# Six column groups of the projections put ahead of attention, and the row blocks in another order

## The chip, the core and the metric

The kernel runs on one core of a Trainium2 chip. The metric is the device time of one execution in microseconds, the median of the runs shown. The engines are TensorE (PE in the profile; PEld are its weight loads), VectorE (DVE), ScalarE (ACT), GpSimd (POOL) and SyncE (SP), which here only issues DMAs; 16 DMA engines move data.

## What is computed

One step of a hybrid decoder layer for a prompt of 1024 tokens and eight tokens to decode. The input is normed and projected; the columns of the projection go to three mixers (sparse attention, causal pooling, a chunked gating MLP), each has a SiLU gate, and one output projection follows.

```python
q, kc, ks, kw, gl, za, pin, zb, u, v, zc = project(rms_norm(xp, norm_pre[l]), w_in[l])
ya = nsa_attend(q, gates, kc, ks, kw, ...)          # compressed + selected + window branches, ALiBi
yb = pool_mix(pin, zeros, 0, pool_w[l], pool_scale[l])
yc, vn = gmlp_mix(u, v, gmlp_norm[l], gmlp_ws[l], gmlp_bs[l], CHUNK)
mix = concat([ya * silu(za), yb * silu(zb), yc * silu(zc)])
xp = xp + rms_norm(mix @ w_out[l], norm_post[l])
```

The same is done for the eight decoded tokens against paged caches.

## The kernel before

All arithmetic that needs float32 precision is done in float16 halves: a value is held as a high part and a low part, and each product is three matmuls (high by high, low by high, high by low).

**Column groups.** `tgroup(gi, ...)` (L538) projects 128 columns of w_in for all 1032 tokens: three pieces (344 tokens each) of 24 matmuls. Its `prefetch` makes the halves of the next group's weights (`split_w`, L255 on ScalarE; the low half at L261 on VectorE, or at L258 and L259 on GpSimd once attention has begun) and loads those of the group after (`load_w`, L243, on SyncE; one `raw` buffer). After a group its `post_...` steps run on the other engines: `post_silu` (gates), `post_u` and `gmlp` (the MLP, with matmuls of its own), `post_pin` (pooling, mostly on GpSimd; it loads `dsh` from the pool state at L1126, copies the last eight columns into it on ScalarE at L1162 and stores it by `o_ps` at L1163) and `poolmm`.

**Stages.** The first 250 us hold the projections for attention and the decoding of the eight tokens, in which `weave` alternates chunks of a group with chunks of side work. Then comes attention over the prompt. Six groups are left for it: ZC1, U1, PIN1, ZB1, PIN0 and ZB0.

**Attention.** A row block is 128 queries; block i has 8 heads and needs i + 1 tiles of keys in the selected branch and up to 5 in the window. A unit is one head (of blocks 7 to 3), two (2, 1) or four (0). For each unit: scores on TensorE (tile s), the table and the row maximum on VectorE (L1344, tile P), exp on ScalarE (L1346), the high half H (L1348, ScalarE), the low half L (L1362, VectorE), a transposing DMA for each half on SyncE (L1355 for H, L1363 for L, both into tile T), and three units later the product with the values on TensorE (tile O). There are 2 buffers each of P, H and L, and 3 of T. When a block's eight heads are through, `combine` and `finish` merge the branches, a transposing DMA puts the result into `qa` (L1432), and `outproj` (tiles op) multiplies it by w_out: 48 matmuls of 512 columns for each block.

**What sets the order.** The loop over units asks `take` for fill: chunks of `side` and `fill` on TensorE, as many as a budget from PARAM's s1 and s2 allows. `fill` holds the six groups in turn, then `early_wo` and `open_out`, which free the projections' memory and load and split w_out (`load_wo` L1467 on GpSimd, `split_wo` L1492 and L1493), then the output projections. `side` holds the MLP, the pooling matmuls and `dec_out`, the output projection of the decoded tokens (tiles dops, do, dor). A scheduler orders the instructions of TensorE, VectorE and ScalarE; SyncE and GpSimd issue in the order of the program (`manual_schedule`). Each engine works through its own instructions in order.

Of the kernel before, what the change touches and what calls it, by code (L numbers as in the profile page):

```python
# [42 lines left out]
NCE = _lay(CE, [("ident", 128), ("bones", 128), ("tril", 128), ("oneh", 8), ("td", 520), ("tcd", 64),  # L43
                ("gsel", 24), ("nsl", 1)])
NCD = _lay(CD, [("gpre", 8), ("gpost", 8), ("psc", 2), ("gn", 2), ("ws0", 2), ("bs0", 2)])
PARAM = {"s1": 6.2, "s2": 0.52, "banks": 2, "gp": "-", "p0": 4.0, "p1": 4.0, "p2": 3.0, "p3": 2.5, "lone": 2, "lsp": -1, "tw": 512}
NCX = 128 + 256 + 256


# [1 line left out]
def tile_hymba(ctx: ExitStack, tc: tile.TileContext, A: dict):  # L51
# [54 lines left out]
    now = [0.0]  # L106
# [431 lines left out]
    def tgroup(gi, scale, post, raw=False):  # L538
        while busy(2):
            yield 0, None  # L540
        grab()
        prefetch(gi)
        ws = wsp[gi]
        t = t32(f"t{gi}")
        for c in range(3):
            ps = fp.tile([128, 512], F32, tag="f", name=f"ps{gi}_{c}")[:, :CH]
            for k in range(8):
                t_mms(ps, ws, c, k, k == 0, k == 7)

            def done(c=c, ps=ps):  # L550
                if raw:
                    S.activation(t[:, c * CH:c * CH + CH], ps, AF.Copy, scale=scale)
                else:
                    evac(t, ps, c, scale)
                if c == 2:
                    return fin() if raw else post(t)

            def fin():
                while "R" not in hold:
                    yield  # L560
                V.tensor_tensor(t, t, R, ALU.mult)
                post(t)
            yield 3.5, done
# [27 lines left out]
    def prep(kind, b):  # L591
# [3 lines left out]
        S.activation(hl[:, 0], xf, AF.Copy)  # L595
        (G if kind in PARAM["gp"] else V).tensor_tensor(hl[:, 1], xf, hl[:, 0], ALU.subtract)
        chl[kind, b] = hl
# [440 lines left out]
    def dec_mix():  # L1038
        need("zd0", "zd1", "zd2", "zd3")
        t = yzd  # L1040
        for k in range(2):
            a = k * 64
            V.tensor_tensor(t[a:a + 64], oda[a:a + 64].rearrange("p (b k g) -> p k g b", k=2, g=4)[:, k],
                            yzd[a:a + 64], ALU.mult)
        V.tensor_scalar(t, t, 2.0 ** -11, None, ALU.mult)
        hilo(md[:, 0], md[:, 1], t)
        yield 0, None


    def post_silu(nm):  # L1050
        def f(t):
            while busy():
                yield
            grab()
            y = t32(f"y{nm}")
            S.activation(y, t, AF.Tanh, scale=0.5)
            yield
            if nm[1] == "b":
                V.scalar_tensor_tensor(y, y, 1.0, t, ALU.add, ALU.mult)
            else:  # L1060
                G.tensor_scalar(y, y, 1.0, None, ALU.add)
                G.tensor_tensor(y, y, t, ALU.mult)
                yield from until(later(4.0))
            grab(-1)
            yield
            hold[nm] = y
        return f

    def post_u(f2):
        def f(t):  # L1070
            while f"zc{f2}" not in hold:
                yield
            G.tensor_tensor(t, t, hold.pop(f"zc{f2}"), ALU.mult)  # L1073
            grab(-1)
            yield from until(later(2.3))
            hold[f"w{f2}"] = t
        return f

    def gmlp(f2):
        yield from wait("vn", f"w{f2}")  # L1080
        while busy():
            yield 0, None
        grab()
        yc = t32(f"yc{f2}")
        def fin():
            V.tensor_scalar(yc[:, 1024:NT], vnd[:, f2], ccd("ws0")[:, f2:f2 + 1], ccd("bs0")[:, f2:f2 + 1],
                            ALU.mult, ALU.add)
            G.tensor_tensor(yc, yc, hold.pop(f"w{f2}"), ALU.mult)
            grab(-1)
            yield from until(later(2.3))  # L1090
            yield
            m = mxg[f2] = C.tile([128, 2, NT], F16, tag=f"mxg{f2}", name=f"mxg{f2}")
            S.activation(m[:, 0], yc, AF.Copy)
            G.tensor_tensor(m[:, 1], yc, m[:, 0], ALU.subtract)
            grab(-1)
            yield from until(later(3.3))
            hold[f"mxg{f2}"] = 1

        for h in range(2):
            ps = fp.tile([128, 4, 128], F32, tag="f", name=f"gp{f2}{h}")  # L1100
            for n4 in range(4):
                n = h * 4 + n4
                for a, b in ((0, 0), (1, 0), (0, 1)):
                    for g2 in range(2):
                        g = f2 * 2 + g2
                        mm(ps[g2 * 64:g2 * 64 + 64, n4], vnh[:, a, n, g * 64:g * 64 + 64],
                           wst[:, b, g * 128:g * 128 + 128], a + b == 0, b == 1)

            def done(h=h, ps=ps):
                y4 = yc[:, h * 512:h * 512 + 512].rearrange("p (n i) -> p n i", i=128)  # L1110
                V.scalar_tensor_tensor(y4, ps, 1.0 / 64, bst[:, f2].unsqueeze(1).to_broadcast([128, 4, 128]),
                                       ALU.mult, ALU.add)
                if h == 1:
                    return fin()
            yield 1.4, done
# [65 lines left out]
    def poolmm(f2):  # L1181
        yield from wait(f"dh{f2}", f"zb{f2}")
        mxp = hold["mx"]
        hl = mxp[:, f2]
        y = hold.pop(f"zb{f2}")
        w = wpl[:, :, f2 * 128:f2 * 128 + 128]
        def fin():
            S.activation(mxp[:, f2, 0], y, AF.Copy)
            G.tensor_tensor(mxp[:, f2, 1], y, mxp[:, f2, 0], ALU.subtract)
            grab(-1)  # L1190
            yield from until(later(3.3))
            hold[f"mxp{f2}"] = 1

        for c in range(3):
            ps = fp.tile([128, 512], F32, tag="f", name=f"pp{f2}{c}")[:, :CH]
            c0 = c * CH
            mm(ps, w[:, 0], hl[:, 0, c0:c0 + CH], True, False)
            mm(ps, w[:, 0], hl[:, 1, c0:c0 + CH], False, False)
            mm(ps, w[:, 1], hl[:, 0, c0:c0 + CH], False, True)

            def done(c=c, c0=c0, ps=ps):
                V.scalar_tensor_tensor(y[:, c0:c0 + CH], ps, psc2[:, f2:f2 + 1], y[:, c0:c0 + CH],
                                       ALU.mult, ALU.mult)
                if c == 2:
                    return fin()
            yield 0.45, done
# [10 lines left out]
    def weave(main, side, per):  # L1217
        owed = 0.0
        while True:
            c = chunk(main)  # L1220
            if c is None:
                return
            bg_step()
            if copies and now[0] > 75:
                cwin_copy(*copies.pop(0))
            owed += c
            while side and owed >= per:
                owed -= per
                if chunk(side[0]) is None:
                    side.pop(0)  # L1230
                    continue
                bg_step()
# [11 lines left out]
    for n in range(32):  # L1244
        page(n // 4, n % 4)
    side = [small(), dec_cmp()]
    weave(tgroup(G_KWV, 1.0 / 64, lambda t: post_v(1, t), raw=True), side, PARAM["p0"])
    for g in range(4):
        weave(group_q(g), side, PARAM["p1"])
    flush()  # L1250
# [30 lines left out]
    def load_qx(i, hf):  # L1281
        t = qx[i, hf] = AT.tile([128, 2, 128], F16, tag="qx", name=f"qx{i}{hf}", bufs=2)
        for k in range(2):
            Y.dma_start(t[64 - k * 64:128 - k * 64], qa[k * 64:k * 64 + 64, i, hf * 4 + k:hf * 4 + 4:2])

    ROWS = (7, 6, 2, 1, 0, 5, 4, 3)
    load_qx(ROWS[0], 0)

    def spans(i):
        n = min(i + 1, 5)  # L1290
# [148 lines left out]
    def open_out():  # L1439
        X.release()  # L1440
        outp["O"] = tc.alloc_tile_pool(name="O", bufs=1, side="left", reuse_waits="tile")
        outp["one"] = outp["O"].tile([128, 128], F32, name="one2")
        G.memset(outp["one"], 1.0)
        bg.append(split_wo())
        yield 0.1, None

    def early_wo():
        load_wo(0)
        yield 0.1, None
# [173 lines left out]
        units += [(i, s, nh) for s in range(0, 8, nh)]  # L1623
    fill = []

    side = []

    def take(budget):
        banks = 0
        c = 0  # L1630
# [10 lines left out]
        while budget > 0 and fill and banks < PARAM["banks"]:  # L1641
# [4 lines left out]
            if c == 0:  # L1646
# [2 lines left out]
            budget -= c  # L1649
        return min(budget, 0.0)  # L1650

    fill += [tgroup(G_ZC1, 1.0 / 64, post_silu("zc1")), tgroup(G_U1, 1.0 / 128, post_u(1)),
             tgroup(G_PIN1, 1.0 / 64, post_pin(1)), tgroup(G_ZB1, 1.0 / 64, post_silu("zb1")),
             tgroup(G_PIN0, 1.0 / 64, post_pin(0)), early_wo(), tgroup(G_ZB0, 1.0 / 64, post_silu("zb0")),
             open_out()]
    side += [dec_mix(), gmlp(0), gmlp(1), poolmm(1), poolmm(0), dec_out()]
    pend = {}
    n = len(units)
    owed = 0.0
# [199 lines left out]
```

## Time and profile before

| | |
|---|---|
| median of 3 runs | 588.2 us (587.95 to 589.18) |
| profiled execution | 585.29 us, its span 583.5 us |
| mean granted TensorE clock | 0.953 |
| busy share of the span | PE 89%, PEld 59%, DVE 76%, ACT 55%, POOL 34% |

Times in the profile are microseconds from the start of the span. A stretch is given with the busy time of each engine in it, the granted TensorE clock as a share of 2.4 GHz, and the mean busy share of the 16 DMA engines. Matmuls are pipelined, so the distance from start to start tells more of one than its own duration.

### The profile page before, as it was taken

The page shows a single profiled execution, that of the slowest core. Times are in us where ns is not written, and L with a number is a line of the kernel's source. Part 1 is how long each engine was busy: PE and PEld are TensorE (multiplying, and loading weights), DVE is VectorE, ACT ScalarE, POOL GpSimd, SP SyncE. Part 2 cuts the span into 40 slices and gives each one's busy share as a digit, 9 for nine tenths or more (in the row PEclk, how much of TensorE's full clock was granted, in tenths as well). Part 3 has the DMA queues.
Part 4 walks back from the last instruction along what each step waited for, and adds up shares of the span by engine and source line. Part 5 has one row for each costly group of instructions (what it writes and reads, how often), then busy time and mean ns, then how long its engine had stood idle before and what let it go on. Part 6 is the DMA issues. An engine that isn't in the chain of part 4 may idle for free. (4 is left out here: it accounts for less than half of the span.)

```text
span 583.5 us, 14199 instructions
## 1 busy us (share of the span) xinstructions
PE 519.7 (89%) x5716; PEld 342.7 (59%) x5716; DVE 441.8 (76%) x747; ACT 323.8 (55%) x574; POOL 197.0 (34%) x157
## 2 busy tenths in 40 slices
PE   5889988899999999899999979674599999998974
PEld 3566655589768999666666545442355455454531
DVE  5986489996686667478986987896799788768741
ACT  6444145564553434439656756496487765756600
POOL 1893179403267000045929775132011010000000
PEclk9989999899999999999999998967589999999997
DMA  8613984855675112847898597999969999998952
GB/s 300 260 37 99 253 222 135 244 165 143 206 260 159 39 40 34 239 92 145 171 184 166 97 184 114 125 229 224 124 100 166 182 213 206 177 215 153 199 154 80
DMA packets 199428, 95.31 MB, mean 163 GB/s; under 512 B 168890, under 2 KB 187738, under 8 KB 199362
## 3 DMA queue, kind: packets, MB, share of 16 engines
q1 hardware_dynamic: 195474, 80.85, 65.2%
q0 software_dynamic: 3744, 13.29, 7.3%
q8 instruction: 44, 0.72, 0.5%
q10 hardware_dynamic: 144, 0.26, 0.1%
q14 instruction: 22, 0.18, 0.1%
HBM read 45.43 MB, written 11.86 MB: 98 GB/s over the span
## 5 line engine op out<-in xcount | busy, mean ns | idle before, releaser
L67 PE MATMUL ps<-xh,ws 128*128 128x344 f16 x768 | 175.7, 313 | 5.8 <-DVE t L492 4.3
L67 PEld LDWEIGHTS <-ws 128*128 128x128 f16 x1376 | 129.3, 100 | 87.3 <-issue 17.4
L1346 ACT ACTIVATE P<-P,sm 128x640 f32<-128x640 f32 (+7 forms) x128 | 92.8, 725 | 77.6 <-DVE sm L1344 77.2
L67 PE MATMUL ps<-xl,ws 128*128 128x344 f16 x384 | 120.0, 313 | 0.0
L1362 DVE SCALAR_TENSOR_TENSOR L<-P,H 128x1024 f16<-128x1024 f32 (+4 forms) x50 | 85.0, 1700 | 25.7 <-ACT H L1348 15.3
L1344 DVE CUSTOM_DVE_ANT_0 P<-s,ctt 128x640 f32<-128x640 f32 (+7 forms) x128 | 84.8, 699 | 13.2 <-PE s L67 12.7
L67 PE MATMUL O<-vn,T 128*128 128x64 f16 x1584 | 64.0, 198 | 26.3 <-DMA T<-L 17.1
L67 PEld LDWEIGHTS <-T 128*128 128x128 f16 x1584 | 57.6, 101 | 40.4 <-DMA T<-L 18.9
L67 PEld LDWEIGHTS <-qa 128*128 128x128 f16 (+1 forms) x612 | 44.7, 98 | 61.5 <-issue 33.5
L1348 ACT ACTIVATE H<-P 128x1024 f16<-128x1024 f32 (+4 forms) x50 | 66.3, 1325 | 1.1
L67 PEld LDWEIGHTS <-xh 128*128 128x128 f16 x768 | 60.3, 98 | 0.7
L67 PE MATMUL op<-wo,qa 128*128 128x512 f16 x192 | 46.4, 389 | 3.3 <-DMA qa<-yza 3.3
L67 PE MATMUL s<-ka,qa 128*128 128x384 f16 (+4 forms) x192 | 45.1, 324 | 3.9 <-DVE sm L1344 3.7
L67 PE MATMUL zps<-ws,xh 128*128 128x128 f16 x512 | 45.0, 219 | 0.0
L1534 POOL TENSOR_SCALAR sq<-sq 128x1 f32<-128x1 f32 x8 | 3.9, 492 | 119.4 <-ACT o L1565 119.4
L67 PE MATMUL zps<-ws,xl 128*128 128x128 f16 x256 | 43.6, 219 | 0.0
L67 PEld LDWEIGHTS <-xl 128*128 128x128 f16 x384 | 37.5, 98 | 1.1 <-issue 0.5
L255 ACT ACTIVATE ws<-raw 128x1024 f16<-128x1024 f32 x21 | 22.2, 1056 | 17.6 <-PE ps L67 12.2
L67 PE MATMUL s<-kl,qa 64*128 64x384 f16 (+5 forms) x100 | 30.2, 329 | 0.0
L67 PE MATMUL s<-klx,qx 64*128 64x384 f16 (+4 forms) x92 | 26.9, 323 | 0.0
L1073 POOL TENSOR_TENSOR t<-t,yzc 128x1032 f32<-128x1032 f32 x2 | 4.8, 2382 | 60.4 <-DVE t L492 60.4
L67 PE MATMUL op<-wo,mxg 128*128 128x512 f16 x96 | 24.8, 395 | 0.1
(333 smaller groups left out, 917.5 us busy)
## 6 DMA issues: line engine op xcount, KB each, us to landing
raw<-in_wt_dram SPq DMA_DIRECT2D x21, 512.0 KB, 4.5
wor<-in_wo_dram POOLq DMA_DIRECT2D x8, 512.0 KB, 7.3
xr<-in_xn_dram SPq DMA_DIRECT2D x8, 512.0 KB, 4.8
o_y_dram<-o SPq DMA_DIRECT2D x7, 512.0 KB, 3.9
cr<-in_ccmp_dram SPq DMA_DIRECT2D x24, 128.0 KB, 3.3
o_kww_dram<-in_cwin_dram POOLq DMA_DIRECT2D x8, 259.0 KB, 4.5
o_kww_dram<-in_cwin_dram POOLq DMA_DIRECT2D x8, 252.0 KB, 4.8
xq<-in_xT_dram SPq DMA_DIRECT2D x3, 516.0 KB, 7.6
```

The source lines that it names most:

```text
L67: nc.tensor.matmul(out, lhsT=l, rhs=r, start=st, stop=en)
L255: S.activation(ws[:, 0, :, a:b], r, AF.Copy, scale=64.0)
L1073: G.tensor_tensor(t, t, hold.pop(f"zc{f2}"), ALU.mult)
L1344: V.tensor_tensor_reduce(p, ps[:, z:z + T], ctt[:, end - T:end], -slope, 3e38, ALU.add, ALU.min, sm[:, s, br:br + 1])
L1346: S.activation(p, p, AF.Exp, bias=sm[:, s, br:br + 1], scale=-1.0, accum_out=sm[:, s, 2 + br:3 + br])
L1348: S.activation(H, P, AF.Copy, scale=1024.0)
L1362: V.scalar_tensor_tensor(L, P, 1024.0, H, ALU.mult, ALU.subtract)
L1534: G.tensor_scalar(sq[:, 2:3], sq[:, 1:2], 1.0 / 1024, sq[:, 0:1], ALU.mult, ALU.add)
```

## The change

The six groups are woven with their side work behind decode, ahead of the loop over units, and no longer handed to `fill`. The row blocks come in another order. PARAM's s1 and s2 are smaller, and `weave` moves its planning clock on when a chunk returned nothing. The number of instructions on each engine stays the same.

```diff
-PARAM = {"s1": 6.2, "s2": 0.52, "banks": 2, "gp": "-", ...}
+PARAM = {"s1": 5.4, "s2": 0.46, "banks": 2, "gp": "-", ...}
...
             owed += c
+            if c == 0:
+                now[0] += 0.5
...
-    ROWS = (7, 6, 2, 1, 0, 5, 4, 3)
+    ROWS = (7, 2, 6, 1, 5, 0, 4, 3)
     load_qx(ROWS[0], 0)
+    side = [dec_mix(), gmlp(0)]
+    weave(tgroup(G_ZC1, 1.0 / 64, post_silu("zc1")), side, 3.0)
+    weave(tgroup(G_U1, 1.0 / 128, post_u(1)), side, 3.0)
+    side += [gmlp(1)]
...
+    weave(tgroup(G_PIN0, 1.0 / 64, post_pin(0)), side, 3.0)
+    weave(tgroup(G_ZB0, 1.0 / 64, post_silu("zb0")), side, 3.0)
+    side += [poolmm(0)]
...
-    fill += [tgroup(G_ZC1, 1.0 / 64, post_silu("zc1")), tgroup(G_U1, 1.0 / 128, post_u(1)),
...
-             open_out()]
-    side += [dec_mix(), gmlp(0), gmlp(1), poolmm(1), poolmm(0), dec_out()]
+    fill += [early_wo(), open_out()]
+    side += [dec_out()]
```

What it moves, first on SyncE where attention begins (raw13 to raw17 are weights of groups, T7_0 the transposed tile of block 7's first head). Before:

```order
L1284 DMA qx70_3989<-qa_87 64x2x128 x2
L1284 DMA qx71_3994<-qa_87 64x2x128 x2
L1355 DMA_TRANSPOSE T7_0_4013<-H7_0_4011 128x13x128
L243 DMA raw16_4024<-in_wt_dram 128x1024
L1363 DMA_TRANSPOSE T7_0_4013<-L7_0_4096 128x13x128
L1355 DMA_TRANSPOSE T7_1_4099<-H7_1_4094 128x13x128
```

and now:

```order
L1286 DMA qx70_3989<-qa_87 64x2x128 x2
L243 DMA raw16_3996<-in_wt_dram 128x1024
L243 DMA raw17_4117<-in_wt_dram 128x1024
L243 DMA raw14_4229<-in_wt_dram 128x1024
L243 DMA raw15_4345<-in_wt_dram 128x1024
L1126 DMA dsh1_4545<-in_stT_dram 128x8x15
L1163 DMA o_ps_dram<-dsh1_4545 1024x1x15
L1126 DMA dsh0_4578<-in_stT_dram 128x8x15
L1163 DMA o_ps_dram<-dsh0_4578 1024x1x15
L1286 DMA qx71_4705<-qa_87 64x2x128 x2
L1369 DMA_TRANSPOSE T7_0_4724<-H7_0_4722 128x13x128
L1377 DMA_TRANSPOSE T7_0_4724<-L7_0_4754 128x13x128
```

All loads of weights and both rounds of dsh and o_ps now stand ahead of the first transpose.

Second, on VectorE where w_out is split (wo, with wor what was loaded; P1 and P6 are scores of row blocks 1 and 6, L2 the low half of block 2). Before:

```order
L1493 SCALAR_TENSOR_TENSOR wo5_6223<-wor5_5967,wo5_6223 128x1024
L1412 RECIPROCAL as2_1_6096<-as2_1_6096 128x8
L1362 SCALAR_TENSOR_TENSOR L2_6_5872<-P2_6_5735,H2_6_5754 128x1536
L1168 SCALAR_TENSOR_TENSOR sd0_6050<-sd0_6050,cpt_81,t14_5215 128x8
L1493 SCALAR_TENSOR_TENSOR wo4_6226<-wor4_5969,wo4_6226 128x1024
L1344 ISA P1_2_5938,sm1_5848<-s1_2_0_5939,ctt_82 128x256
```

and now:

```order
L1507 SCALAR_TENSOR_TENSOR wo2_4989<-wor2_4799,wo2_4989 128x1024
L1507 SCALAR_TENSOR_TENSOR wo3_4992<-wor3_4804,wo3_4992 128x1024
L1614 TENSOR_TENSOR do32_5251<-do32_5251,dops_5056 128x64
L1624 TENSOR_REDUCE dor_5368<-dops2_5327 128x8
L1625 TENSOR_SCALAR dor_5368<-dor_5368 128x8
L1628 TENSOR_TENSOR do32_5251<-do32_5251,dor_5368 128x64
L1629 TENSOR_TENSOR do32_5251<-do32_5251,cdt_83 128x64
L1630 TENSOR_TENSOR do32_5251<-do32_5251,dsq_5252 128x64
L1358 ISA P6_0_5605,sm6_5606<-s6_0_0_5610,ctt_82 128x896
```

The splits stood among the units of blocks 2 and 1, with dec_out's steps much later, in block 5; now they stand in a row with dec_out's steps behind them, and the first scores of block 6 come after.

## Rows read from the trace of the kernel before

**Rows 1.** The page: busy us, share of the span, instructions.
```profile
PE 519.7 (89%) x5716; PEld 342.7 (59%) x5716; DVE 441.8 (76%) x747; ACT 323.8 (55%) x574; POOL 197.0 (34%) x157
```

**Rows 2.** Blocks 7, 6, 2, 1, 0, 5, 4, 3, tail: us, PE, PEld, DVE, ACT, POOL, clock, DMA, GB/s.
```profile
256.70:307.40 50.70, 50.70 (x603) 33.05 (x601) 43.78 (x58) 32.67 (x46) 28.27 (x11) 1.00 0.88 168
307.40:364.20 56.80, 50.28 (x584) 32.52 (x581) 45.84 (x77) 36.79 (x61) 42.16 (x29) 0.97 0.79 140
364.20:396.00 31.80, 23.06 (x234) 13.87 (x233) 28.32 (x58) 23.13 (x48) 8.65 (x9) 0.79 0.97 164
396.00:425.60 29.60, 14.53 (x161) 8.86 (x160) 20.79 (x68) 17.95 (x50) 1.88 (x4) 0.61 0.95 169
425.60:437.30 11.70, 11.70 (x174) 6.93 (x172) 11.00 (x32) 10.11 (x28) 2.50 (x1) 0.95 0.77 123
437.30:479.60 42.30, 40.25 (x467) 21.65 (x464) 35.98 (x65) 29.81 (x54) 4.17 (x5) 1.00 1.01 185
479.60:522.30 42.70, 42.70 (x425) 22.02 (x423) 33.23 (x61) 27.47 (x53) 2.14 (x4) 1.00 1.04 197
522.30:555.90 33.60, 32.07 (x303) 16.61 (x303) 25.20 (x50) 20.32 (x43) 2.06 (x4) 1.00 0.96 179
555.90:583.50 27.60, 15.75 (x106) 7.17 (x104) 8.11 (x12) 2.69 (x7) 1.61 (x4) 0.88 0.42 117
```

**Rows 3.** The same view: first to last transpose of attention, and two stretches.
```profile
256.70:555.90 299.20, 265.28 (x2933) 155.49 (x2931) 244.15 (x461) 198.25 (x375) 91.83 (x65) 0.93 0.92 169
380.00:400.00 20.00, 14.93 (x150) 8.80 (x148) 19.40 (x36) 17.98 (x37) 8.72 (x8) 0.69 0.96 201
400.00:427.00 27.00, 13.09 (x133) 8.18 (x134) 18.19 (x60) 16.21 (x44) 0.40 (x1) 0.56 0.89 156
```

**Rows 4.** Tile dsh: durations (ns, least, median, most), first and last start.
```profile
L1162 ACT ACTIVATE dsh<-t x2: 200/208/215, 308.3 to 378.7; 128x8 f32<-128x8 f32 x2
```

**Rows 5.** Timeline of PE at attention's begin: start us, us, what.
```profile
251.90 0.32 PE L67 MATMUL ps<-xh,ws 128*128 128x344 f16 x1
...
258.90 0.87 PE L67 MATMUL s<-ka,qa 128*128 128x512 f16 x4
...
260.51 1.53 PE L67 MATMUL gp<-wst,vnh 128*64 128x128 f16 x48
```

**Rows 6.** VectorE's groups by shape, 251 to 584: busy us, mean ns, idle before.
```profile
L1362 DVE SCALAR_TENSOR_TENSOR L<-P,H 128x1664 f16<-128x1664 f32 x8 | 20.1, 2511 | 2.1 <-ACT H L1348 2.1
L1344 DVE CUSTOM_DVE_ANT_0 P<-s,ctt 128x1024 f32<-128x1024 f32 x8 | 9.7, 1214 | 1.4 <-PE s L67 1.4
L1344 DVE CUSTOM_DVE_ANT_0 P<-s,ctt 128x640 f32<-128x640 f32 x40 | 32.3, 816 | 2.3 <-PE s L67 2.1
L492 DVE SCALAR_TENSOR_TENSOR t<-ps,R 128x344 f32<-128x344 f32 x18 | 9.1, 506 | 1.5 <-PE ps L67 1.5
L1493 DVE SCALAR_TENSOR_TENSOR wo<-wor,wo 128x1024 f16<-128x1024 f32 x8 | 10.6, 1337 | 1.2 <-ACT wo L1492 1.2
```

**Rows 7.** Timeline of SyncE's queue: the first transpose of attention.
```profile
256.71 1.53 SPq L1355 DMA_TRANSPOSE T<-H  x1
```

**Rows 8.** GpSimd's groups by line, 251 to 430: the low halves of weights.
```profile
L258 POOL TENSOR_SCALAR raw<-raw 128x1024 f32<-128x1024 f32 x5 | 15.5, 3105 | 9.3 <-issue 8.5 <-POOL yc L1088 0.8
L259 POOL TENSOR_TENSOR ws<-raw,ws 128x1024 f16<-128x1024 f32 x5 | 11.2, 2249 | 0.4
```

**Rows 9.** Timeline of GpSimd: the last loads of w_out.
```profile
395.75 1.62 POOL L1467 DMA_DIRECT2D wor<-in_wo_dram  x3
```

**Rows 10.** Timeline of VectorE: the last two splits of w_out.
```profile
410.68 2.35 DVE L1493 SCALAR_TENSOR_TENSOR wo<-wor,wo 128x1024 f16<-128x1024 f32 x2
```

**Rows 11.** Busy times in a stretch of block 5.
```profile
460.00:480.00 20.00, 19.21 (x208) 10.14 (x208) 16.75 (x28) 12.30 (x24) 1.66 (x2) 1.00 1.07 207
```

## What the change was predicted to do

> **What bounds the kernel now.** I read the busy shares first, then the span cut into attention's row blocks, then the timelines at the places that the change touches. TensorE is busy for 89% of the span and VectorE for 76% [rows 1]. The cut by row blocks (each stretch runs from the first transpose of a block's high half, T<-H, to that of the next one) says more [rows 2]. In block 7 TensorE is busy for 50.70 of 50.70 us: the column groups woven in there leave it no gap. In block 4, filled by output projections, it is 42.70 of 42.70. But VectorE is close behind: 43.78, 45.84 and 28.32 us in blocks 7, 6 and 2, and over all of attention 244.15 of 299.20 us, 82%, beside TensorE's 265.28 us, 89%, with the DMA engines at 0.92 [rows 3]. So attention is a stage in which TensorE, VectorE and the transposing DMAs are nearly matched, and the six column groups are the work with which TensorE fills it. The hole is blocks 2, 1 and 0: 73.1 us in which TensorE works for 49.3 [rows 2], at a granted clock of 0.56 between 400 and 427 [rows 3].
>
> **Part 1: the groups go ahead of attention.** Nothing before 251.5 us moves. The instruction order shows what does. On SyncE, which issues in program order, the first transpose T<-H of row block 7 stood behind two small loads; now four weight loads and both pairs of dsh load and o_ps store stand ahead of it. The second o_ps store needs ScalarE's copy of the last columns of PIN0's result (0.2 us, [rows 4]), and so the fifth group must be through TensorE before any attention transpose is issued. TensorE may still pull row 7's score matmuls forward (the order has four heads and six matmuls of the fifth among the groups), but without transposes these stop when two H tiles are full.
>
> How long the hold is: with nothing between, 48 matmuls of a group take 258.90 - 251.90 = 7.0 us, 0.146 us each [rows 5], so five groups of 72 take 52.6 us. Four gMLP pieces of 24 at 1.53/48 us each are 3.1 us. Eight score matmuls took 1.6 us (258.90 to 260.51, [rows 5]); 37 of them are in the order ahead of PIN0's end, 6 to 7 us. That puts PIN0's end at 251.9 + 62 = 314; VectorE's last copy (0.5 us, [rows 6]), the 0.2 us on ScalarE and three issues on SyncE make 316. Before, the same transpose went out at 256.71 [rows 7]. **The hold costs 59 us.** GpSimd could make it longer: it makes the low halves of the weights, 3.1 + 2.2 us for each of five groups [rows 8], in order with gMLP's steps; I add about 47 us of its work in a stage of 62 and find each split 3 to 4 us ahead of its matmuls, so I price that wait at nothing, with 10 us as the other end (about one gap between groups for each of three splits).
>
> **Part 2: what attention gets for it.** From the first to the last transpose it took 299.2 us [rows 3]. VectorE's work there and in the 5 us ahead is 248 us. Of that the new stage takes over only what it can reach: 15 copies of 0.506 us, four heads' P (1.21 + 0.82 us each), two L of 2.5 us [rows 6], some 7 us of gMLP and gates, 28 us in all. **220 us of VectorE work are left behind the hold**, while VectorE was idle for over half of the 62 us in it. To break even attention would have to run in 299.2 - 59 = 240 us, VectorE at 92%. Its mean was 82%; it reached 97% once, for 20 us [rows 3]. Block by block:
> - Block 7: 50.7 us before, bound by TensorE. Now some 29 us of VectorE work (six L, four P, ZB0's copies, the pooling), plus 4 to 5 us in which the first pair of transposes lands: 35.
> - Block 2 now comes second and holds w_out and dec_out. In the order row 6's first P stands on VectorE behind all eight wo splits and the six steps of dec_out. Before, the last three loads went out at 395.75 and their splits ended at 413.0, 17 us later [rows 9, 10]. Now all eight follow one another behind GpSimd's mxp step, some 6 us into the block, two of them only after the first splits: 23 us, then dec_out's 128 small matmuls and its chain over ScalarE, GpSimd and VectorE, 10 us, then P, exp and H: 42. Before, blocks 2, 1 and 0 together took 73.1 us; now 42 + 18 + 12 = 72, blocks 1 and 0 by their VectorE work without w_out (20.79 less its splits of 1.3 us each, and 11.00, [rows 2, 6]).
> - Block 6: 56.8 before. It loses its three groups and gains the output projections of rows 7 and 2. VectorE and TensorE then both need about 40: 43.
> - Blocks 5, 4 and 3 already ran with output projections as fill (42.3, 42.7, 33.6 us, [rows 2]). Row 4's fill stays about as large, row 3's shrinks: 41, 40, 30.
>
> Sum: 316 + 35 + 42 + 43 + 18 + 41 + 12 + 40 + 30 = 577, plus the tail behind the last transpose, the same chain as before, 27.6 us [rows 2]: a span of 604.6 us against 583.5, 21 us more. VectorE's share in the new attention would be 220/261, 84%, a little better than before, since TensorE crowds it less. The profiled run took 585.29 us and lies 2.9 us under the median of 588.2, so I add the difference to the median: **609 us**. For this mechanism alone I give 596 to 620: attention between 248 us (VectorE at 89%) and 272 us (81%).
>
> **Part 3: the order of the row blocks and the planner's numbers.** With 7, 2, 6, 1, 5, 0, 4, 3 each small block stands between two large ones, so that a short block's output projection falls beside a long block's transposes. That is in the sum. s1 and s2 only set how much fill the plan takes for each unit; the fill is now output projections alone.
>
> **The rivals.**
> *Faster.* Attention freed of the groups runs at the best pace of the trace: VectorE at 97% as between 380 and 400 [rows 3]. 220/0.97 = 227 us, 316 + 227 + 27.6 = 571, on the median's scale 575. The DMA would allow nearly that: 169 GB/s over 299.2 us is 50.6 MB, less four weights of 0.5 MB; at 207 GB/s, the best 20 us that I looked at [rows 11], 234 us. For it: the hole at half clock could close. Against it: row 6's first P has the whole of dec_out ahead of it, and 97% has to hold for 227 us.
>
> *TensorE has room in the stage of groups.* The weight loads were busy for only 33.05 of block 7's 50.70 us [rows 2]. If that share were the true load, the groups packed together would need 0.65 of their 52.6 us, the hold would be 18 us shorter, and the time 591; with a slightly better pace in attention no change. Against it: 0.146 us for 344 columns is 2.36 GHz at a column each cycle, so the groups already run at the full clock's rate [rows 5]. The Trainium skill, in Perfetto Trace Analysis, Identifying the Most-Contended Engine, calls the matmul busy share a poor measure and wants the share of weight loads instead; by that rule this rival would hold, by the spacing in the trace it does not.
>
> *The clock falls.* Between 400 and 427 TensorE was busy about half the time and was granted 0.56, mostly the 1.2 GHz level [rows 3]. Blocks 7 and 2 now leave it idle for some 40% of 77 us. If it runs at 1.2 GHz there, its 45 us become up to 75 and end what VectorE ended before: 10 to 15 us more, 619 to 624.
>
> *GpSimd ends the groups late* (part 1): 10 us more, 619.
>
> That the change does not do what it says is not open for SyncE, whose order is fixed; on TensorE the pulled scores are counted.
>
> **How the numbers follow.** Forecast 0.62. Faster 0.11. Room in the groups 0.06, about half of it within 0.2%. Clock 0.13, GpSimd 0.08. Two runs of this kernel can be told apart from about 0.2% on, 1.2 us. Slower by more: 0.62 + 0.13 + 0.08 + 0.02 = 0.85; same 0.04; faster 0.11. The range leaves out the faster case and the last few per cent of the clock's: 590 to 623.
>
> **What would show it right or wrong.** The first T<-H near 316 us and nothing on the DMA engines for most of the 60 us before; VectorE under half busy there; row 6's first P waiting for dec_out; 250 to 270 us from the first to the last transpose. If the first transpose comes before 300, or attention takes under 240 us, I am wrong; if the clock column shows a half-speed stretch between 320 and 390, the clock's case is the one.

## The result and the profile after

The changed kernel takes 636.4 us (median of 631.5 to 639.2) against 588.7 us: 1.079 times before, 95% interval 1.070 to 1.088. In a second set of runs it was 1.093 (1.086 to 1.101). Some executions take over 1.5% longer than their kernel's fastest; the ratios leave these out, the medians do not. The loss is 48 us by these medians, where 21 were predicted, and the time lies above the range of 590 to 623.

The stretches of the changed kernel show where it went, cut as in [rows 2]. The columns are from:to, length, then busy us (and instructions) of PE, PEld, DVE, ACT and POOL, the granted clock, the DMA share and GB/s. The first is the stage of the six groups. Then come blocks 7, 2, 6, 1, 5, 0, 4, 3 and the tail, then all of attention from its first to its last transpose.

```profile
256.70:320.60 63.90, 63.65 (x500) 40.60 (x499) 31.33 (x49) 20.41 (x30) 47.91 (x25) 1.00 0.15 38
320.60:364.20 43.60, 30.64 (x387) 18.87 (x384) 33.53 (x61) 30.29 (x49) 19.74 (x18) 0.86 0.95 155
364.20:413.80 49.60, 32.87 (x357) 17.65 (x356) 34.30 (x58) 27.68 (x47) 12.47 (x14) 0.64 0.75 175
413.80:462.50 48.70, 41.34 (x443) 22.17 (x442) 35.52 (x64) 28.69 (x54) 1.64 (x4) 0.93 0.97 175
462.50:479.50 17.00, 13.15 (x154) 7.29 (x155) 13.85 (x38) 12.84 (x31) 0.00 (x0) 0.90 0.91 166
479.50:524.40 44.90, 39.94 (x419) 21.63 (x418) 33.86 (x69) 30.02 (x62) 1.61 (x4) 0.92 0.93 180
524.40:535.50 11.10, 9.41 (x82) 4.82 (x82) 9.11 (x31) 8.52 (x25) 0.00 (x0) 0.58 0.66 114
535.50:580.20 44.70, 40.19 (x395) 20.78 (x394) 34.97 (x62) 27.20 (x52) 1.61 (x4) 0.95 0.90 168
580.20:611.30 31.10, 25.68 (x283) 13.65 (x282) 22.93 (x47) 20.02 (x41) 0.80 (x2) 0.95 0.96 170
611.30:637.50 26.20, 10.32 (x53) 4.16 (x51) 6.32 (x10) 2.00 (x5) 0.81 (x2) 0.70 0.33 90
...
320.60:611.30 290.70, 233.21 (x2512) 126.85 (x2510) 218.07 (x424) 185.25 (x353) 37.87 (x45) 0.86 0.90 168
```

The first transpose of attention leaves at 320.6 us instead of 256.7 [rows 7]: 63.9 us later. In return attention, relieved of six groups, takes 290.7 us instead of 299.2 [rows 3]: 8.5 us. The tail is 1.4 us shorter. 63.9 - 8.5 - 1.4 = 54.0 us, the difference of the two spans (637.5 and 583.5). So the hold came about as foreseen and attention gave little back. The head of the changed kernel's profile agrees: TensorE has the same 5716 matmuls in a longer span, busy for 85% of it instead of 89% [rows 1].

```profile
PE 543.9 (85%) x5716; PEld 351.1 (55%) x5716; DVE 442.5 (69%) x747; ACT 326.4 (51%) x574; POOL 187.3 (29%) x157
```

Block 2 has a gap of its own. SyncE's queue in the timeline of the changed kernel (start, us, what):

```profile
369.43 7.30 SPq L1369 DMA_TRANSPOSE T<-H  x1
399.09 0.37 SPq L1631 DMA_DIRECT2D o_yd_dram<-do  x1
399.56 1.25 SPq L1286 DMA_DIRECT2D qx<-qa  x2
400.86 1.54 SPq L1377 DMA_TRANSPOSE T<-L  x1
```

From the start of the second T<-H to the next issue it is 29.7 us: the store of the decode outputs, o_yd, stands in the queue ahead of block 2's second T<-L, and dec_out must first be through all its engines. VectorE shows the same place: the low half for that T<-L, ready at 370.1 us, then its last step of dec_out, then the first P of row 6. From the end of the T<-H's issue, at 376.7, the transpose stood behind the store for 24 us.

```profile
368.34 1.76 DVE L1376 SCALAR_TENSOR_TENSOR L<-P,H 128x1536 f16<-128x1536 f32 x1 [0.30 <-DMA T<-L]
...
398.84 0.23 DVE L1630 TENSOR_TENSOR do<-do,dsq 128x64 f32<-128x64 f32 x1
401.94 1.09 DVE L1358 CUSTOM_DVE_ANT_0 P<-s,ctt 128x896 f32<-128x896 f32 x1 [2.88 <-PE s L67]
```

### The profile page after: what moved, and what is told of

Read it like the earlier page. It is cut to its first block, busy times and chain, and to the rows that moved or that the text cites. A ratio compares the mean times of both kernels' runs of the same rounds, so it can differ in the third digit from the quotient of the medians.

```text
span 637.5 us, 14201 instructions
## 1 busy us (share of the span) xinstructions
PE 543.9 (85%) x5716; PEld 351.1 (55%) x5716; DVE 442.5 (69%) x747; ACT 326.4 (51%) x574; POOL 187.3 (29%) x157
## 4 chain that ended last, share of the span: by engine, by line
PE 46%; DMA 16%; DVE 15%; SPq 7%; issue 7%; ACT 6%; POOL 2%; DVEq 0%; POOLq 0%; ACTq 0%
PE ps L67 15%; PE op L67 10%; DMA T<-L 7%; PE zps L67 5%; PE s L67 4%; DMA T<-H 4%; PE O L67 4%; ACT P L1360 2%; PE v1ps L67 2%; DVE P L1358 2%; DVE L L1376 2%; SPq L311 2%; DMA xq<-in_xT_dram 1%; DMA qa<-yza 1%; SPq L318 1%
## 5 line engine op out<-in xcount | busy, mean ns | idle before, releaser
L67 PE MATMUL ps<-xh,ws 128*128 128x344 f16 x768 | 173.3, 311 | 5.1 <-DVE t L492 3.3
L67 PEld LDWEIGHTS <-ws 128*128 128x128 f16 x1376 | 129.8, 99 | 85.2 <-issue 15.5
L1376 DVE SCALAR_TENSOR_TENSOR L<-P,H 128x1024 f16<-128x1024 f32 (+4 forms) x50 | 81.7, 1636 | 27.6 <-DMA T<-L 17.0
L67 PE MATMUL O<-vn,T 128*128 128x64 f16 x1584 | 70.4, 203 | 35.1 <-DMA T<-L 22.7
L67 PEld LDWEIGHTS <-qa 128*128 128x128 f16 (+1 forms) x612 | 46.8, 101 | 82.5 <-issue 46.4
L67 PEld LDWEIGHTS <-T 128*128 128x128 f16 x1584 | 60.3, 104 | 52.9 <-DMA T<-L 26.4
L67 PEld LDWEIGHTS <-xh 128*128 128x128 f16 x768 | 61.2, 99 | 0.7
L67 PE MATMUL op<-wo,qa 128*128 128x512 f16 x192 | 49.2, 418 | 10.2 <-DMA qa<-yza 10.2
L67 PE MATMUL s<-ka,qa 128*128 128x384 f16 (+4 forms) x192 | 48.9, 347 | 6.2 <-DVE sm L1358 6.2
L67 PE MATMUL zps<-ws,xl 128*128 128x128 f16 x256 | 43.6, 219 | 0.0
L67 PE MATMUL s<-klx,qx 64*128 64x384 f16 (+4 forms) x92 | 30.5, 347 | 5.4 <-DMA qx<-qa 5.2
L67 PE MATMUL s<-kl,qa 64*128 64x384 f16 (+5 forms) x100 | 33.2, 352 | 0.0
L492 DVE SCALAR_TENSOR_TENSOR t<-ps,R 128x344 f32<-128x344 f32 x30 | 15.2, 511 | 24.1 <-PE ps L67 23.8
```

The costliest lines, as they stand in the source:

```text
L67: nc.tensor.matmul(out, lhsT=l, rhs=r, start=st, stop=en)
L492: V.scalar_tensor_tensor(t[:, c0:c0 + CH], ps, scale, R[:, c0:c0 + CH], ALU.mult, ALU.mult)
L1376: V.scalar_tensor_tensor(L, P, 1024.0, H, ALU.mult, ALU.subtract)
```

## The experiments

Every time below is a median; a ratio is to the kernel before, measured beside it (583.9 to 589.0 us there). L1.. are lines of the changed kernel. "Attention" is the time from the first to the last transpose in the profiled run.

**Which part of the change costs.** order_only is the kernel before with one line changed:

```
-    ROWS = (7, 6, 2, 1, 0, 5, 4, 3)
+    ROWS = (7, 2, 6, 1, 5, 0, 4, 3)
```

> The kernel before with the new order of the row blocks alone (7, 2, 6, 1, 5, 0, 4, 3); the six groups stay in attention as fill. My theory: the loss comes from the groups' place, the order alone is worth little: 583 to 596 us, against 588.7 of before. Rival A (the order is the loss: with block 2 second, w_out and the decode outputs come at a bad place): over 605 us.

Measured: 591.9 us, 1.013 (1.009 to 1.018), as expected.

groups_only is the changed kernel with that line turned back.

> The changed kernel with the old order of the row blocks (7, 6, 2, 1, 0, 5, 4, 3); the six groups stay ahead of attention. My theory (hold of the transposes, little given back): 628 to 645 us, first T<-H at about 320 us as in the changed kernel. Rival A (the order is the loss): under 615 us.

Measured: 641.9 us, 1.095 (1.084 to 1.106), the first T<-H at 320.5.

planner_only is the kernel before with the two numbers:

```
-PARAM = {"s1": 6.2, "s2": 0.52, ...
+PARAM = {"s1": 5.4, "s2": 0.46, ...
```

> The kernel before with the planner's two numbers of the changed one alone (s1 5.4, s2 0.46); groups in attention, old order. I hold them for small: 0.99 to 1.01 times before. If they carry part of the loss: over 1.015.

Measured: 585.9 us, 0.998 (0.995 to 1.002): nothing. So the groups' place is the loss. The order of the blocks alone costs about 1%, and with the groups ahead the old order is no faster (rival A falls); the planner's numbers cost nothing. Attention in groups_only:

```profile
320.50:614.50 294.00, 228.95 (x2515) 125.47 (x2512) 219.31 (x424) 185.63 (x353) 35.74 (x45) 0.86 0.87 167
```

**Fewer groups.** two_groups leaves ZC1 and U1 ahead of attention and puts the other four back into the fill:

```
-    weave(tgroup(G_PIN1, ...), side, 3.0)
...
-    weave(tgroup(G_ZB0, ...), side, 3.0)
+    fill += [tgroup(G_PIN1, ...), tgroup(G_ZB1, ...), tgroup(G_PIN0, ...), early_wo(), tgroup(G_ZB0, ...), open_out()]
+    side += [gmlp(1), poolmm(1), poolmm(0), dec_out()]
```

> The changed kernel with only ZC1 and U1 ahead of attention; PIN1, ZB1, PIN0 and ZB0 stay in attention as fill, the new order of the row blocks stays. My theory (the price is the time by which the first transposes come later, 10 to 11 us a group, and little is given back): first T<-H at 275 to 285 us, time 15 to 22 us above the kernel with the new order alone, 607 to 614 where before takes 584. Rival E (the price is not by group but a single step, the stall of block 2 behind the decode outputs): within 6 us of the kernel with the new order alone, 588 to 598.

Measured: 616.1 us, 1.052 (1.044 to 1.060), the first T<-H at 280.0, both as the price by group wanted, so rival E falls. But attention took 307.3 us, longer than before's although two groups had left it (the new order has an unknown part in that):

```profile
280.00:587.30 307.30, 252.69 (x2789) 144.36 (x2786) 237.35 (x451) 194.10 (x370) 75.69 (x62) 0.93 0.94 165
```

Beside order_only's 1.013 and the changed kernel's 1.079 to 1.093, the first two of the six groups carry about half of the loss.

one_group puts ZC1 alone ahead, in the old order.

```
+    side = [dec_mix(), gmlp(0)]
+    weave(tgroup(G_ZC1, 1.0 / 64, post_silu("zc1")), side, 3.0)
...
-    fill += [tgroup(G_ZC1, 1.0 / 64, post_silu("zc1")), tgroup(G_U1, 1.0 / 128, post_u(1)),
+    fill += [tgroup(G_U1, 1.0 / 128, post_u(1)),
```

> The kernel before with one group, ZC1, and its gMLP pieces ahead of attention, five as fill, old order, old numbers: the price of one group at the smallest dose. If each group costs its time ahead and gives little back: first T<-H 10 to 13 us later, 1.010 to 1.020 times before. If TensorE is so full in block 7 (50.7 of 50.7 us) that a group taken out there gives back all of its time: within 0.5% of before or faster.

Measured: 605.3, 614.9, 615.1 and 616.0 us against a median of 587.7. The fastest is 1.030 times before; no interval can be given. Both expectations were too low. The trace is of the execution of 614.9 us: its first T<-H left at 271.4 us, 14.7 later than before [rows 7], and it does not show what the fastest one paid. How attention gets longer with one group or two ahead is open.

**The hold on SyncE.** hold_free lets GpSimd issue what stood ahead of the transposes:

```
-            Y.dma_start(raw, A["wt"][gi])
+            (G if "attn" in hold else Y).dma_start(raw, A["wt"][gi])
...
-            Y.dma_start(dsh[:, :, 0:15], A["stT"][f2])
+            G.dma_start(dsh[:, :, 0:15], A["stT"][f2])
...
-                    Y.dma_start(A["o_ps"][f2], dsh[:, :, 1:16])
+                    G.dma_start(A["o_ps"][f2], dsh[:, :, 1:16])
```

> The changed kernel with the groups' weight loads, the dsh loads and the o_ps stores issued by GpSimd instead of SyncE, so that nothing but the two small loads stands ahead of the first T<-H. My theory (the hold on SyncE is the price): first T<-H at 270 to 275 us instead of 320.6; three or four of block 7's eight heads get through while the groups run, 15 to 22 us gained: 613 to 622 us. Rival D (TensorE, full with the groups, is what keeps attention from starting; the queue is only the messenger): the first T<-H comes early, but the time stays within 6 us of 636.

Measured: 653.3 us, 1.116 (1.106 to 1.125), slower still. SyncE's queue and TensorE in its timeline:

```profile
272.96 1.54 SPq L1369 DMA_TRANSPOSE T<-H  x1
...
291.32 1.53 SPq L1377 DMA_TRANSPOSE T<-L  x1
321.88 1.46 SPq L1369 DMA_TRANSPOSE T<-H  x1
...
345.94 2.15 SPq L1369 DMA_TRANSPOSE T<-H  x1
367.12 0.36 SPq L1610 DMA_DIRECT2D dsq<-in_xTs_dram  x1
```

```profile
299.50 0.35 PE L67 MATMUL O<-vn,T 128*128 128x64 f16 x6
...
320.92 0.89 PE L67 MATMUL O<-vn,T 128*128 128x64 f16 x25
```

The first T<-H leaves at 273.0, and three pairs get out. Then SyncE stands until 321.9: there are three T buffers, and the matmuls that read the first (O<-vn,T) stand in TensorE's order in pieces between the groups, the last at 320.9. That is rival D's mechanism: TensorE, not the queue alone, keeps attention from going on. Its number did not come, as the time is not within 6 us of 636. The edit also makes a new wait, so it does not price the hold by itself: GpSimd reaches PIN0's dsh load and o_ps only at 344 and 361.5 us, and dec_out's small load (dsq), which shares that tile, holds SyncE from 345.9 to 367.1.

**The stall in block 2.** dec_late:

```
     fill += [early_wo(), open_out()]
-    side += [dec_out()]
...
                 fill.append(outproj(v[0]))
+                if v[0] == 1:
+                    side.append(dec_out())
```

> The changed kernel with the output projection of the decode tokens (dec_out) queued only when row block 1 is done, instead of right at the start of attention. In the trace of the changed kernel SyncE issued nothing from 369.4 to 399.1 us: the store of the decode outputs (o_yd) stood in its queue ahead of the second T<-L of block 2. Theory B (this one wait is a good part of why attention did not get shorter): block 2 falls from 49.6 to 25 to 32 us, some 3 us come back in block 5, time 612 to 622 us. Rival C (attention runs at a pace of its own, the later blocks take back what block 2 saves): 630 to 638 us.

Measured: 630.9 us, 1.078 (1.068 to 1.087); attention 280.6. Its block 2 and its attention:

```profile
364.60:395.50 30.90, 20.51 (x213) 10.29 (x213) 22.46 (x42) 24.51 (x42) 9.61 (x14) 0.80 1.05 260
321.80:602.40 280.60, 224.20 (x2515) 122.36 (x2512) 215.15 (x424) 185.15 (x353) 37.58 (x45) 0.90 0.92 174
```

Block 2 saves 18.7 us, as theory B said, but attention only some 10: blocks 6, 1, 5 and 3 give about half of it back, which is rival C. By medians the gain is not separated from the changed kernel's spread. The edit takes away the wait on SyncE and dec_out's work on TensorE and VectorE together, so it does not price the queue alone.

**Which resource sets attention's pace.** The yardstick first:

> The changed kernel once more, on the chip of the other runs of this call, as their yardstick: 1.07 to 1.09 times before, about 630 us where before takes 584.

Measured: 640.4 us, 1.093; attention 289.7 us. The ratio is a little above the 1.07 to 1.09 expected; the two sets of the changed kernel differ by 1.3%.

no_low_transpose drops the second transpose and lets TensorE read the high half twice; no_low_subtract drops VectorE's subtraction and transposes H twice:

```
-        Y.dma_start_transpose(out=pt[:, nh * nt:2 * nh * nt], in_=L.rearrange("p h c -> p (h c)"))
...
-                    mm(o, pt[:, nh * nt + q], vn[br][:, kt, c], False, last)
+                    mm(o, pt[:, q], vn[br][:, kt, c], False, last)
```

> The changed kernel without the transposes of the low halves (T<-L); the subtraction that makes L stays on VectorE, and TensorE's matmuls stay, reading the high half twice (the output lacks the low part). Theory T (the transposing DMAs set attention's pace; their queue moved 5.6 to 5.8 tiles of 128x128 a us at most, and 2112 tiles leave 290 us little room): attention falls from 291 to 235 to 250 us, time 40 to 55 us below the changed kernel. Theory V (VectorE's 218 us of work set it, as the prediction had it): within 8 us of the changed kernel. Theory P (TensorE's order sets it): within 10 us as well.

```
-        V.scalar_tensor_tensor(L, P, 1024.0, H, ALU.mult, ALU.subtract)
-        Y.dma_start_transpose(out=pt[:, nh * nt:2 * nh * nt], in_=L.rearrange("p h c -> p (h c)"))
+        Y.dma_start_transpose(out=pt[:, nh * nt:2 * nh * nt], in_=H.rearrange("p h c -> p (h c)"))
```

> The changed kernel without VectorE's subtraction L<-P,H (about 80 of its 218 us in attention); the same transposes, the second of each pair reading H again, and the same matmuls (the output lacks the low part). Theory V (VectorE sets the pace): attention 40 to 60 us shorter. Theory T (the transposing DMAs): within 10 us of the changed kernel. Theory P (TensorE): within 10 us.

Measured: 617.4 us, 1.053 (1.045 to 1.061), and 632.4 us, 1.078 (1.069 to 1.087). (Here and in bare_attention the expectation counts the tiles twice over: 66 x 8 heads x 2 halves are 1056.) Attention in the first, its block 7, and attention in the second:

```profile
320.40:588.40 268.00, 214.08 (x2453) 119.31 (x2452) 212.35 (x421) 184.61 (x351) 40.54 (x43) 0.90 0.57 119
...
320.40:357.70 37.30, 29.24 (x419) 19.35 (x418) 28.99 (x54) 26.12 (x40) 18.92 (x16) 0.91 0.57 99
```

```profile
323.80:605.90 282.10, 222.28 (x2480) 122.07 (x2478) 147.91 (x375) 182.99 (x353) 30.84 (x45) 0.87 0.92 173
```

VectorE falls from 216 to 148 us, and attention shortens by 7.6: theory V falls. Half of the transposes are worth 21.7, which is half of what theory T wanted and twice what theory P allowed: none of the three holds alone.

The same edit in the kernel before:

> The kernel before without the transposes of the low halves (the low part is left out of the output; VectorE's and TensorE's work stays). Theory T' (in the kernel before, TensorE, full with the groups, set the pace of blocks 7 and 6, and the transposes were hidden behind it; only without the groups do they come to the front): blocks 7 and 6 stay within 3 us each, the whole kernel 0 to 12 us faster than before. Theory T'' (the transposes set attention's pace in both kernels): 20 to 30 us faster than before, blocks 7 and 6 each 5 us or more shorter.

Measured: 579.5 us, 0.985 (0.980 to 0.990). Blocks 7 and 6:

```profile
259.10:310.60 51.50, 51.24 (x604) 33.23 (x602) 43.66 (x58) 32.90 (x46) 27.30 (x11) 1.00 0.54 101
310.60:365.70 55.10, 50.07 (x590) 32.04 (x588) 46.10 (x76) 36.17 (x59) 41.55 (x29) 0.97 0.43 86
```

They stay at 51.5 and 55.1 us (before 50.7 and 56.8, [rows 2]) though half of the transposes are gone. T' holds: in the kernel before the groups on TensorE hid the transposes there; in the changed kernel block 7 without low transposes falls from 43.6 to 37.3.

dec_late_no_low_transpose joins two of the edits.

> The changed kernel with dec_out queued after row block 1 and without the transposes of the low halves (the low part is left out of the output; VectorE's and TensorE's work stays). Apart, the first edit took 9 us off attention and the second 22. Theory T+B (the stall of block 2 behind the decode outputs and the pace of the transposing DMAs are the two things that kept attention from shortening): together 30 to 45 us off the changed kernel's 290, attention 245 to 260, time 1.01 to 1.03 times before (changed kernel: 1.08 to 1.09). Theory P (a pace that neither of them sets): the two don't add, attention stays above 265 us.

Measured: 617.2 us, 1.051 (1.045 to 1.056), attention 269.1: the same as no_low_transpose alone (268.0), as theory P said. The two don't add: block 2 is 8.8 us shorter than there, and the later blocks give it back.

double_scores gives TensorE more to do:

```
-                    mm(ps[:, a:a + w], qa[:, i, s], ka[br][:, k, c0:c0 + w], True, False)
+                    mm(ps[:, a:a + w], qa[:, i, s], ka[br][:, k, c0:c0 + w], True, True)
+                    mm(ps[:, a:a + w], qa[:, i, s], ka[br][:, k, c0:c0 + w], True, False)
```

> The changed kernel with the first of the two passes of every score matmul issued twice (the second overwrites the first, the output is the same): some 26 to 28 us more TensorE work in attention at the full clock, worked out from 0.146 us for 344 columns and 67,600 columns. Theory T (TensorE has room): 0 to 8 us slower than the changed kernel. Theory P (TensorE, by its order or its load, sets the pace): 15 to 30 us slower. Rival K (the clock that falls for lack of work is the loss; more work keeps it up): 5 us or more faster, granted clock in attention over 0.92 instead of 0.87.

Measured: 652.1 us, 1.109 (1.104 to 1.115); attention:

```profile
319.20:618.70 299.50, 244.64 (x2685) 138.12 (x2683) 219.04 (x424) 186.16 (x353) 37.16 (x45) 0.91 0.86 163
```

The added matmuls, 28 us by the estimate above, cost 10 in attention, between T and P; TensorE's busy time there rose by 15.5 us. The granted clock rose from 0.87 to 0.91 and the kernel got slower, so rival K's gain did not come, though the clock did not reach the 0.92 that it named. Block 7 alone became 2 us shorter.

**Attention bare.** bare_attention queues every projection and dec_out behind the last row block:

```
-    side += [dec_out()]
+    after = []
...
-                fill.append(outproj(v[0]))
+                after.append(outproj(v[0]))
...
+    fill += after
+    side.append(dec_out())
     while fill or side:
```

> The changed kernel with all output projections and dec_out queued only behind the last row block: attention runs with no fill but w_out's loads and splits; the tail gets all eight projections (some 70 to 90 us more there). What attention's own pace is, without the groups and without the projections. Theory T (the transposing DMAs alone set it, at 5.7 tiles of 128x128 a us): 1056 pairs of tiles, 2112 tiles less what overlaps nothing, 190 to 215 us from the first to the last transpose. Theory V (VectorE, as predicted: some 195 us of work without the projections' 25 us, at 84%): 225 to 240 us. Theory P (blocks of projection matmuls and the landings of the transposes take turns; without the projections the turns are gone): well under 261, no more exact than T or V. Theory C (the chain of one unit, P, exp, H, transpose, with two or three buffers, sets it, whatever the fill): 265 us or more.

Measured: 636.7 us, 1.087 (1.078 to 1.096): no different from the changed kernel. Its attention and its tail; below, attention in the second profile of the changed kernel:

```profile
318.90:560.00 241.10, 176.73 (x2216) 103.97 (x2214) 197.44 (x400) 177.46 (x331) 32.23 (x33) 0.79 0.99 174
560.00:634.20 74.20, 66.61 (x349) 30.64 (x348) 23.06 (x34) 9.26 (x27) 5.64 (x14) 0.97 0.40 126
```

```profile
319.40:609.10 289.70, 229.15 (x2515) 124.43 (x2512) 216.35 (x424) 185.15 (x353) 35.73 (x45) 0.87 0.90 169
```

This reading decides most. Woven into attention, the projections and dec_out lengthen it by 289.7 - 241.1 = 48.6 us. Put behind it, they lengthen the tail by 74.2 - 26.1 = 48.1 us. In the changed kernel the fill hides nothing. In the kernel before some of it was hidden: there groups, projections and dec_out together made attention 299.2 - 241.1 = 58.1 us longer than the bare one, and in the changed kernel and the bare one this work apart takes 63.9 + 48.1 = 112 us (37 of row 7's scores included). The difference, 54 us, is that of the two spans. Block by block the 48.6 are 0.6 in block 7, 19.7 in block 2 (most of it the decode outputs, by dec_late), 5.5 in 6, 3.4 in 1, 5.5 in 5, 0.2 in 0, 9.3 in 4 and 4.4 in 3.

Of the theories V came nearest, with 225 to 240 us, and P asked only for well under 261; T and C fall. The next three kernels test V and T again.

Three more bare kernels, without the low transposes, without the subtraction, and without both (edits as above):

> The same without the transposes of the low halves (the low part is left out of the output). Theory T: attention at least 30 us shorter than in the bare kernel. Theory V: within 8 us of it. Theory C: 10 to 25 us shorter, since a landing leaves each unit's chain.

> The kernel with bare attention (no projections, no dec_out in it) without VectorE's subtraction L<-P,H (about 75 of its 197 us there); each second transpose reads H again, so the transposes and the matmuls stay (the low part is left out of the output). Theory T (the transposing DMAs, busy 0.99 of bare attention, set its pace): attention within 10 us of the bare 241. Theory V (VectorE, 82% busy there, sets it): 195 to 215 us.

> Bare attention without the subtraction and without the transposes of the low halves (the low part is left out of the output). If transposes and VectorE are matched, each hidden behind the other, only both together shorten it: 175 to 205 us instead of 241 (ScalarE's 177 us are then the next). If the chain of one unit through all engines sets the pace whatever the loads: over 215 us.

Measured: 633.3 us (1.079), 634.9 us (1.083) and 610.7 us (1.043; 1.037 to 1.050). Attention in the three:

```profile
317.00:554.10 237.10, 167.54 (x2202) 101.15 (x2201) 196.58 (x398) 176.86 (x329) 33.18 (x33) 0.83 0.62 105
```

```profile
320.30:563.00 242.70, 179.38 (x2228) 106.53 (x2226) 131.32 (x352) 174.29 (x331) 26.29 (x33) 0.81 0.99 173
```

```profile
320.40:530.20 209.80, 155.44 (x2169) 95.04 (x2167) 130.00 (x350) 171.68 (x329) 26.18 (x33) 0.85 0.67 119
```

Each alone is worth 4 us or nothing, both together 31: transposes and VectorE's work each stand behind the other. That is the matched pair the last expectation named, though at 210 us attention lies between the two ranges given there. The pair shows in blocks 5 and 4, which take 73.8 us bare, 70.0 and 71.1 with one edit, and 52.9 with both. There ScalarE (the fourth busy time of a row) is next, at 49.8 us of the 52.9:

```profile
442.50:470.00 27.50, 19.53 (x300) 12.21 (x299) 16.55 (x52) 25.79 (x53) 0.00 (x0) 0.88 0.80 129
...
484.00:509.40 25.40, 21.17 (x391) 13.10 (x387) 17.13 (x47) 23.97 (x46) 1.68 (x1) 1.00 0.84 130
```

Block 6 does not follow: 42.7 us bare and 50.7 with both edits. The pair does not account for that, and its cause is not shown.

**A try at a faster kernel.** before_row5 puts block 5 ahead of the small blocks in the kernel before, ROWS = (7, 6, 5, 2, 1, 0, 4, 3).

> The kernel before with row block 5 pulled ahead of the small blocks (7, 6, 5, 2, 1, 0, 4, 3), groups still as fill. Before, blocks 2, 1 and 0 took 73 us with TensorE working for 49 of them, while w_out was loaded and split. If the last groups and w_out fall beside block 5, whose transposes take long, the small blocks run without them: 3 to 10 us faster than before. If the hole only moves (block 5 grows by what the small ones save): within 3 us of before. If block 5's P and L wait behind the wo splits on VectorE: up to 8 us slower.

Measured: 599.4 us, 1.016 (1.010 to 1.023). Blocks 2, 1 and 0 took 63 us instead of 73, but block 5 took 61.2 instead of 42.3: the hole moved and grew. No kernel here that computes everything beats the one before.

## Why the prediction was wrong

**The hold was right.** First T<-H predicted for 316, seen at 320.6 and, in the second profile, 319.4. In the stage TensorE worked 63.65 of 63.90 us and VectorE 31.33, about half, as said. GpSimd's splits did not end it. But SyncE's order was not the only thing that held block 7: with the queue freed, in hold_free, three heads got out and the fourth waited for TensorE.

**Room in the groups fell.** That rival wanted the weight loads' share, here 40.60 of 63.90 us, to be the true load of TensorE; the 500 matmuls filled the stage without a gap. The Trainium skill, in Perfetto Trace Analysis, Identifying the Most-Contended Engine, sets two measures in place of the matmul busy share: that share, and the flops done as a share of the peak. The prediction named only the first, which misled here at 64%; the spacing of 0.146 us for 344 columns [rows 5] stands for the second, and by it the stage had no room.

**The clock's case came about, and nothing shows it as the cause.** The clock did fall in blocks 7 and 2 (0.86 and 0.64), as that rival wanted. But dec_late brings block 2 from 49.6 to 30.9 us without adding work there, and its clock from 0.64 to 0.80, so the low clock came with the waiting; double_scores, with a higher clock in attention, is slower, and bare attention, at 0.79, is shorter. No run changes the clock alone.

**The faster case did not come.** It wanted 227 us of attention.

**The step that failed is the sum of attention by VectorE's work.** It gave 261 us, and 290.7 came. It took VectorE's work to set the pace and the fill to run beside it; but 68 us less VectorE work shortened attention by 7.6 (no_low_subtract), and the fill hid nothing (48.6 us in attention, 48.1 behind it). That blocks 1, 0 and 3 came within 1.1 us of the sum does not bear the rule out. Two of its terms were mis-sized:

- The fill was counted only as VectorE work. By the bare kernel VectorE has 197.4 us without projections and decode outputs and 216.4 with them. At the rate of bare attention (197.4 of 241.1, 82%) these 18.9 us would cost 23: 241 + 23 = 264, nearly the forecast. They cost 48.6. They are TensorE's and the queues' work as well, and on TensorE they stand in one order with the scores. The chain of waits of the changed kernel shows this in block 5 (start, us, what):

```profile
484.82 1.25 PE s L67 x4
486.07 6.58 PE op L67 x24
492.65 0.51 PE s L67 x4
...
502.93 5.87 DMA T<-H
508.80 0.05 issue
508.85 0.23 PE O L67 x2
509.08 0.59 PE s L67 x4
509.68 5.35 PE op L67 x24
515.04 0.52 PE s L67 x4
```

  Twenty-four matmuls of a projection stand as one block between the scores of two heads; then attention waits for a transpose to land; then the next block comes. In this stretch they take turns instead of overlapping. That the whole cost comes about in this way is argued from such chains; the runs show the cost, and not that. Blocks 6, 5, 4 and 3, predicted at 43, 41, 40 and 30, took 48.7, 44.9, 44.7 and 31.1.
- Block 7 was put at 35 and took 43.6, and 44.0 bare. There is no projection in it; its transposes set it (37.3 without the low ones, 43.1 without the subtraction). The prediction took its 29 us of VectorE work and the first landing, and no time for the transposes that follow. It saw the DMA share of 0.92 [rows 3] and weighed the DMA only in the faster case, by 207 GB/s, a window in which plain loads and stores made up some 1.5 of 4.1 MB [rows 11].

Block 2's 42 became 49.6. The wait for dec_out was foreseen on VectorE; that its store holds SyncE, and with it block 2's own transposes, was not (24 us for one of them). The remaining differences are 1.4 us or less, and the hold's 4.6.

**What stays open.** Why the first two groups ahead already cost about half of the whole loss; two_groups shows that attention got longer, and not why. Open too is why about half of the fill was hidden in the kernel before and none in the changed one.

## What to carry to other kernels

An engine's busy share says what bounds a stage only if taking work off that engine shortens it: here 66 us less on VectorE, or half of the transposes, changed bare attention by 4 us at most, and both by 31. Before moving work out of a stage as its "fill", ask what it hid there, and what the fill that is left will hide; the cheapest test is to run the stage bare and look whether the total changes. In a queue that issues in program order, look also for the last small store of a side chain: a load or store that nobody waits for can still hold everything queued behind it, though taking that hold away was worth little here as long as attention's pace was set elsewhere.

## What the runs showed of the hardware

The share of the DMA engines is no measure of how much faster they could move things. In the changed kernel they are full in a stretch of transposes and nearly full in one of plain loads (below each, its packets):

```profile
325.00:350.00 25.00, 20.30 (x258) 13.29 (x259) 20.34 (x28) 16.72 (x22) 14.49 (x12) 0.87 1.10 189
DMA packets 18717, 4.73 MB, mean 189 GB/s; under 512 B 18714, under 2 KB 18714, under 8 KB 18714
...
0.00:20.00 20.00, 13.04 (x69) 7.72 (x70) 12.70 (x22) 13.91 (x18) 5.94 (x8) 1.00 0.87 324
DMA packets 2515, 6.49 MB, mean 324 GB/s; under 512 B 283, under 2 KB 939, under 8 KB 2515
```

That is 189 GB/s at a share of 1.10 and 324 at 0.87; the transposes went in packets of some 250 bytes, the loads in packets of 2.6 KB. And bare attention stayed at 0.99 with or without a third of VectorE's work, while with half of its transposes it fell to 0.62 and took 4 us less. The Trainium skill, in VectorE: DVE Perf Modes, The three transpose paths, gives the transposing path about 90% of the DMA bandwidth. These two rows come out lower: 189 of 324 is 58%, for transposes of this shape inside the core's memory beside plain loads from HBM.
